# Softmax denominators behind the value products, and work moved between engines, in the mixers of a hybrid encoder layer

## The chip, the cores and the metric

The kernel runs on one core of a Trainium2 chip. The metric is device microseconds (us) of one execution, the median of several; less is better. A core has five engines with an instruction queue each: PE (matrix products, and transposes as products with the identity), DVE (elementwise and reductions), ACT (activation functions, copies with a scale), POOL (elementwise, and DMAs that accumulate) and SP, which in this kernel only issues DMAs. Each engine takes its instructions strictly in order and waits at semaphores, so an instruction that waits holds up everything behind it on its engine, DMA issues included. PSUM is the memory that PE writes to; here it is used as 8 banks of 128x512 fp32.

## The reference

One post-norm encoder layer over 1024 tokens of width 1024, in fp32. Two mixers share a projection, then come an output product, a norm, a SwiGLU feed-forward and a gated embedding. The part around the change, cut from the reference:

```python
u = x @ w_in                                    # rq, rk, rv, rg | aq, ak, av
kv = einsum('bhnsd,bhnse->bhnde', k * k_decay, v)   # retention, 8 heads, chunks of 128, both directions
...
y_ret = group_norm(y_fwd + y_bwd) * gn_gain * silu(rg)
scores = where(valid, q.k / 8 - slope * dist, -1e30)  # attention, 8 heads, window +-128
m = maximum(max(scores), sink)
e = exp(scores - m)
denom = sum(e) + exp(sink - m)
y_att = (e / denom) @ v
h = LN1(alpha * x + concat(y_ret, y_att) @ w_out)
```

## The kernel before

Every large product is written as three fp32r products of operands that are split into a high and a low part (`mm3`, L75 to L79: high by high, high by low, low by high). A split costs an ACT copy for the high part and a DVE subtraction for the low one (`split`, L69 to L72; `put`, L600 to L604, does both and stores the pair to DRAM).

The span of the profile falls into stages: the first projection (to about 48 us), the mixers (about 48 to 353 us), w_out, which is made as seven products of sums of blocks with operands that lie in DRAM as `wod` (from 353 us), LN1, and the feed-forward with its embedding gate (to the end). The change touches the mixers alone.

In the mixers the order of PE's work is written out by hand. A projection step (`take`) is one `mm3`, that is three 128x512 products; each step is a tick. Between the steps stand the mixers' own small products. `run` (L726) deals the two out against each other: attention group 0 runs first by itself, then retention group 0, then three pairs of a retention and an attention group i = 1, 2, 3, with 48 ticks each. Lists `later` and `side` hold functions that fire at a certain tick, so that work which depends on a result is put into the engines' queues some ticks after it. DVE, ACT, POOL and SP get their instructions in an order that a scheduler sets; `behind` (L81) ties an instruction to a place behind the last product.

A retention group turns its keys (L408), multiplies them with a decay for each direction (`keys`, L411, on DVE, from PSUM to SBUF), makes the chunk states (L428), scans them, scores (L459, L461), values (L481), and norms each half of 512 tokens: `evict` reads the sums out of PSUM (L488 and L489 squares on ACT, L490 a copy on DVE, L491 a subtraction on DVE), L498 sums the squares on PE, L500 makes a row on DVE, and then at 3, 6, 9, 12 and 15 ticks (`LAGS`) the row goes to 64 partitions by DMA (L505), POOL takes a power (L508), the result goes to DRAM (L511), comes back as a broadcast (L515), and DVE multiplies y by it (L519).

An attention group works on blocks of 128 queries, two heads at a time, each against two or three blocks of keys (`nk` = 256 or 384). POOL writes the sink logit into a column behind the scores (L545); PE makes the scores in a bank "s" (L548, L549); DVE scales them, adds the distances and takes the maximum (L550); DVE negates the maximum (L552); ACT takes the exponentials, the sink's column among them, and their sum (L554). Three ticks later (`LAG`) DVE takes the reciprocal of the sum (L558) and ACT multiplies the exponentials by it (L560). Then PE turns them into bank "t" (L572), ACT copies them out (L574, tile `ptr`), PE multiplies them with the values into bank "o" (L584), and after four blocks ACT copies the half out (L587). Banks "s", "t" and "o" are two each, so a product that starts in such a bank waits until the bank's last reader is done.

Beside this `presplit_out` (L606 to L643) makes the operands of w_out: it loads blocks of w_out into SBUF, adds blocks to each other in place on DVE (L638, in the order of the table `todo`), and stores each sum, split, with `put`. `presplit_gate` does the like for other weights (L653, L663).

Of the kernel before, what the change touches and what calls it, by code (L numbers as in the profile page):

```python
# [30 lines left out]
LAG = 3  # L31
# [11 lines left out]
def layer(tc, xT, xn, w_first, w_mt, w_rv, w_out, w_pg, w_pe, pT, w_gu, w_dn,  # L43
# [175 lines left out]
    nlg = cp.tile([P, 16], F32, name="nlg")  # L219
    dve.tensor_tensor(nlg, rr[:, 0:16], t_[:, 0:16], ALU.mult)  # L220
# [23 lines left out]
    def ev_aq(b, qs, h, i):  # L244
        sl = slice(h * HF, (h + 1) * HF)
        for g in range(2):
            sc_ = 0.125 / slope(i, g)
            a = slice(64 * g, 64 * g + 64)
            z = slice(64 * (1 - g), 64 * (1 - g) + 64)
            act.activation(qs[g][a, sl], b[a], AF.Copy, scale=sc_)  # L250
            dve.scalar_tensor_tensor(qs[g][z, sl], b[a], sc_, qs[g][a, sl].bitcast(F32), ALU.mult, ALU.subtract)
# [127 lines left out]
    def decay_k(i, h):  # L379
        e = bt([P, 2, P], "sq", 1)  # L380
        for d in range(2):
            behind(act.activation(e[:, d, :], cst[:, C_BASE + P:C_BASE + 2 * P], AF.Exp,
                                  scale=nlg[:, 8 * d + 2 * i + h:8 * d + 2 * i + h + 1]))
# [9 lines left out]
    class Retention:  # L393
# [8 lines left out]
        def keys(self, q):  # L402
# [7 lines left out]
            for d in range(2):  # L410
                dve.tensor_tensor(  # L411
                    kdec[:, d].rearrange("p n (h e) -> p n h e", h=2),
                    tb.rearrange("p n (h e) -> p n h e", h=2),
                    kd[:, d, 2 * i:2 * i + 2].unsqueeze(1).unsqueeze(3).to_broadcast([P, 4, 2, 64]),
                    ALU.mult)
# [69 lines left out]
        def evict(self, hh):  # L485
# [4 lines left out]
            dve.tensor_copy(self.half(hh), of)  # L490
# [35 lines left out]
    class Attention:  # L526


        def __init__(self, i, y):
            self.i, self.y, self.qs = i, y, pairs[i][2]  # L530
            self.st, self.sc, self.pt, self.o, self.ready = {}, {}, {}, {}, set()

        def scores(self, n):
# [9 lines left out]
            sc = self.sc[n] = [bt([P, NKT + 4], "sc", NSC) for _ in range(2)]  # L543
            for g in range(2):
                pool.tensor_copy(sc[g][:, nk:nk + 1], skb[:, 2 * i + g:2 * i + g + 1])  # L545
            for g in range(2):
# [4 lines left out]
                                         skb[:, 2 * i + g:2 * i + g + 1], ALU.add, ALU.max, st_[:, 0, j, g:g + 1])  # L551
            dve.tensor_scalar(st_[:, 1, j, :], st_[:, 0, j, :], -1.0, None, ALU.mult)  # L552
            for g in range(2):
                act.activation(sc[g][:, :nk + 1], sc[g][:, :nk + 1], AF.Exp, bias=st_[:, 1, j, g:g + 1],  # L554
                               accum_out=st_[:, 2, j, g:g + 1])

            def scaled():
                behind(dve.reciprocal(st_[:, 3, j, :], st_[:, 2, j, :]))  # L558
                for g in range(2):
                    behind(act.activation(sc[g][:, :nk], sc[g][:, :nk], AF.Copy, scale=st_[:, 3, j, g:g + 1]))  # L560
                self.ready.add(n)

            later.append((ticks[0] + LAG, scaled))

        def turn(self, n):
            assert n in self.ready
# [10 lines left out]
        def values(self, n):  # L577
# [8 lines left out]
            if j == 3:  # L586
                act.activation(self.half(hh), self.o[hh], AF.Copy)  # L587
# [6 lines left out]
    rnd = dr.tile([8, P, 8], F32, name="rnd")  # L594
    pgd = dr.tile([7, 4, P, 2, HF], F32, name="pgd")
# [28 lines left out]
    def presplit_out(kt, ops, start, gap, raws=()):  # L624
# [10 lines left out]
        def step(p, k, k2, i):  # L635
            x = hold[k]
            if k2 is not None:
                behind(dve.tensor_tensor(x, x, hold[k2], ALU.add))  # L638
            put(x, ops[i % len(ops)], wod[p - 1, kt])

        todo = ((1, 0, None), (2, 2, None), (3, 3, None), (5, 0, 1), (7, 1, 3), (6, 0, 3), (4, 0, 2))
        return [(ticks[0] + start, load)] + \
            [(ticks[0] + start + 5 + gap * i, lambda i=i, a=a: step(*a, i)) for i, a in enumerate(todo)]  # L643
# [1251 lines left out]
def const_table():  # L1895
# [10 lines left out]
    c[:, C_BASE:C_BASE + NKT] = np.where(d <= P, -d, np.float32(-1e33))  # L1906
# [68 lines left out]
```

## Time and profile before

| | |
|---|---|
| time, median of 3 runs | 1171.35 us (1170.49 to 1171.68) |
| span of the profiled execution | 1166.3 us |
| time around the span (median less span) | 5.05 us |
| PE busy | 1154.7 us, 99% of the span |
| DVE, ACT, POOL busy | 903.6, 576.1, 124.4 us |
| DVE busy in 150:250 us (mixers) | 83.7 of 100 us |
| ACT busy in 150:250 us | 69.8 of 100 us |
| PE's waits for others in the whole span | 3.1 us in four waits |

The profiled execution's own time is taken to be its span and the 5.05 us around it. Starts and durations are in us; an instruction's row gives start, duration, engine, line, operation, and output<-input by the program's names. In brackets stands how long the engine was idle ahead of it and what it waited for. Consecutive 128x512 products of PE overlap: they start 0.23 us apart though each lasts 0.39, so PE can stand still with hardly any idle time in a row; the distance between starts tells more. Rows of the queue view (SPq) are issues of DMAs; a DMA lands some us later.

### The profile page before, as it was taken

Reading aid. Unit: us, or ns where it says so; the run is one execution under the profiler, and the core shown is the slowest. Engines: PE = TensorE matmul, PEld = TensorE weight load, DVE = VectorE, ACT = ScalarE, POOL = GpSimd, SP = SyncE. Lnnn points to the kernel's source line nnn. Section 1 sums busy time; section 2 is a strip of 40 time slices with the busy share of each in tenths; the row PEclk is TensorE's granted clock in tenths of the full one; section 3 lists DMA queues with packets and bytes.
Section 4 is the critical chain, followed back from the end, with each engine's and each line's share of the span. In section 5 each row is a group of like instructions: output and inputs, shape, how many; then the busy total and the mean of one; then the engine's idle time right before and its main releaser. Section 6 shows DMA issues by size and latency. Waiting matters only on the chain.

```text
span 1166.3 us, 17917 instructions
## 1 busy us (share of the span) xinstructions
PE 1154.7 (99%) x6330; PEld 971.3 (83%) x6330; DVE 903.6 (77%) x1746; ACT 576.1 (49%) x1169; POOL 124.4 (11%) x182
## 2 busy tenths in 40 slices
PE   9999999999999999999999999999999999999997
PEld 7888888888887888888888888888888888888885
DVE  5666697877859788948999988889888976864678
ACT  5566358676756265214445433444344445552462
POOL 2001021202010020000000000000000020234243
PEclk9999999999999999999999999999999999999999
DMA  6345676646356955665232232232223289989978
GB/s 253 103 150 205 254 236 215 209 154 218 132 192 231 359 181 197 250 218 197 100 116 92 101 120 103 85 137 99 100 72 136 94 253 350 351 220 225 254 157 234
DMA packets 84377, 214.39 MB, mean 184 GB/s; under 512 B 12224, under 2 KB 17472, under 8 KB 84288
## 3 DMA queue, kind: packets, MB, share of 16 engines
q1 hardware_dynamic: 75504, 195.94, 47.6%
q0 software_dynamic: 8784, 17.31, 8.4%
q8 instruction: 50, 0.82, 0.3%
q14 instruction: 39, 0.32, 0.1%
HBM read 141.32 MB, written 62.16 MB: 174 GB/s over the span
## 4 chain that ended last, share of the span: by engine, by line
PE 94%; DVE 3%; DMA 1%; ACT 1%; issue 1%; POOL 0%; SPq 0%; DVEq 0%; POOLq 0%; ACTq 0%
PE bmm L802 8%; PE bmm L803 8%; PE bmm L804 8%; PE bt L802 6%; PE bt L803 6%; PE bt L804 6%; PE bmm L77 5%; PE bmm L78 5%; PE bmm L79 5%; PE bs L804 4%; PE bs L803 4%; PE bs L802 4%; PE bo L804 4%; PE bo L803 4%; PE bo L802 4%; PE bt L572 2%
## 5 line engine op out<-in xcount | busy, mean ns | idle before, releaser
L77 PE MATMUL bmm<-H,w 128*128 128x512 f32 x240 | 97.0, 404 | 0.0
L78 PE MATMUL bmm<-H,w 128*128 128x512 f32 x240 | 94.1, 392 | 0.0
L79 PE MATMUL bmm<-H,w 128*128 128x512 f32 x240 | 93.9, 391 | 0.0
L1561 POOL DMA_DIRECT2D h0b<-in_w_dn x24 | 21.6, 902 | 538.4 <-DVE ev L1367 503.6
L1387 ACT ACTIVATE ev<-ev 128x512 f32<-128x512 f32 x42 | 26.5, 631 | 103.7 <-DVE ev L1416 90.5
L77 PEld LDWEIGHTS bmm<-H,w 128*128 128x128 f32 x240 | 45.1, 188 | 11.0 <-issue 1.4
L79 PEld LDWEIGHTS bmm<-H,w 128*128 128x128 f32 x240 | 45.0, 188 | 10.2
L78 PEld LDWEIGHTS bmm<-H,w 128*128 128x128 f32 x240 | 45.1, 188 | 8.3 <-DVE H L72 0.4
L554 ACT ACTIVATE sc<-sc,st 128x385 f32<-128x385 f32 (+1 forms) x64 | 37.3, 586 | 27.1 <-DVE st L552 27.0
L550 DVE CUSTOM_DVE_ANT_0 sc<-cst,bs,skb 128x384 f32<-128x384 f32 (+1 forms) x64 | 34.9, 575 | 7.7 <-PE bs L549 7.4
L1416 DVE TENSOR_TENSOR ev<-ev,bt 128x512 f32<-128x512 f32 x44 | 30.1, 684 | 12.6 <-PE bt L804 12.5
L1367 DVE TENSOR_TENSOR ev<-ev,bs 128x256 f32<-128x256 f32 x63 | 25.6, 418 | 15.5 <-PE bs L804 14.7
L545 POOL COPY sc<-skb 128x1 f32<-128x1 f32 x64 | 17.4, 280 | 189.2 <-PE bt L572 163.2
L1389 DVE TENSOR_TENSOR ev<-ev 128x512 f32<-128x512 f32 x42 | 29.0, 691 | 10.6 <-ACT ev L1387 9.1
L802 PE MATMUL bmm<-H,u 128*128 128x512 f32 x92 | 36.1, 392 | 0.0
L803 PE MATMUL bmm<-H,u 128*128 128x512 f32 x92 | 36.0, 392 | 0.0
L804 PE MATMUL bmm<-H,u 128*128 128x512 f32 x92 | 35.8, 389 | 0.0
L71 ACT ACTIVATE H<-ln 128x512 fp32r<-128x512 f32 (+1 forms) x34 | 23.0, 679 | 24.1 <-DVE ln L1051 7.2
L560 ACT ACTIVATE sc<-sc,st 128x384 f32<-128x384 f32 (+1 forms) x64 | 34.2, 583 | 0.9 <-DVE st L558 0.9
L72 DVE TENSOR_TENSOR w<-raw,w 128x512 fp32r<-128x512 f32 x34 | 23.1, 688 | 13.9 <-ACT w L71 13.9
L574 ACT ACTIVATE ptr<-bt 128x384 f32<-128x384 f32 (+1 forms) x64 | 26.6, 458 | 12.9 <-PE bt L572 12.7
L802 PE MATMUL bmm<-H,w 128*128 128x512 f32 x84 | 32.9, 392 | 0.0
(802 smaller groups left out, 3903.0 us busy)
## 6 DMA issues: line engine op xcount, KB each, us to landing
ad<-ev SPq DMA_DIRECT2D x33, 512.0 KB, 2.6
pgd<-pro SPq DMA_DIRECT2D x28, 512.0 KB, 2.9
raw<-in_w_gu SPq DMA_DIRECT2D x22, 512.0 KB, 3.7
ln<-in_w_gu SPq DMA_DIRECT2D x22, 512.0 KB, 3.8
raw<-ad SPq DMA_DIRECT2D x40, 256.0 KB, 5.8
ln<-ad SPq DMA_DIRECT2D x37, 256.0 KB, 6.3
H<-in_w_dn SPq DMA_DIRECT2D x33, 256.0 KB, 7.1
wod<-aq SPq DMA_DIRECT2D x15, 512.0 KB, 2.7
```

The source lines that it names most:

```text
L77: pe.matmul(o, lh, rh, start=start, stop=False)
L78: pe.matmul(o, lh, rl, start=False, stop=False)
L79: recent[0] = pe.matmul(o, ll, rh, start=False, stop=stop).ins.name
L550: dve.tensor_tensor_reduce(sc[g][:, :nk], cst[:, tc0:tc0 + nk], b[:, :nk], slope(i, g), skb[:, 2 * i + g:2 * i + g + 1], ALU.add, ALU.max, ...
L554: act.activation(sc[g][:, :nk + 1], sc[g][:, :nk + 1], AF.Exp, bias=st_[:, 1, j, g:g + 1], accum_out=st_[:, 2, j, g:g + 1])
L560: behind(act.activation(sc[g][:, :nk], sc[g][:, :nk], AF.Copy, scale=st_[:, 3, j, g:g + 1]))
L574: act.activation(p_[:, :hi - lo, :], tb[:, :hi - lo, :], AF.Copy)
L802: pe.matmul(o, lh, rh, start=start, stop=False, skip_group_check=True)
L803: pe.matmul(o, lh, rl, start=False, stop=False, skip_group_check=True)
L804: pe.matmul(o, ll, rh, start=False, stop=stop, skip_group_check=True)
L1389: dve.tensor_tensor(c[:, 1, :], c[:, 0, :], c[:, 1, :], ALU.mult)
L1416: dve.tensor_tensor(get(name), ev[left][:, m, :], right, ALU.add)
```

## The change

Five parts, all in the mixers:

1. The probabilities stay unnormalised. The sink's column goes (64 copies on POOL), and so do the 32 reciprocals of one block and the 64 multiplications on ACT. Instead, once the fourth block of a half has its exponentials, `sums` at +3 ticks adds the exponential of sink less maximum (2 small ACT instructions) to the sums and takes one reciprocal for the four blocks on DVE; `store` at +5 ticks sends the reciprocals to DRAM with two DMAs, each of 128x4 single fp32 elements (L564 of the changed kernel), and `fetch` at +9 ticks brings them back as two broadcasts of 64x512 into the half of y (L568), from where DVE multiplies them with the value products as it empties bank "o" (L593, where ACT copied before). There are eight halves, so 16 stores and 16 fetches.
2. The scores are made with the opposite sign, distances positive and a minimum for the maximum, so that the exponential takes the minimum as it is (scale -1): the 32 negations on DVE go.
3. The keys' decay goes from DVE (16 instructions 128x512) to ACT (32 of 128x4x64, L413 of the changed kernel).
4. `evict` copies on ACT (L488 of the changed kernel) instead of DVE, 8 times.
5. w_out's sums are made by 16 DMAs from POOL's queue that load a block and add it to the tile (L643 of the changed kernel), instead of 16 additions on DVE, in another order of `todo`.

The diff, cut to its core:

```diff
-LAG = 3
+LAGA = (3, 5, 9)
...
-            sc_ = 0.125 / slope(i, g)
+            sc_ = -0.125 / slope(i, g)
...
             for d in range(2):
-                dve.tensor_tensor(
-                    kdec[:, d].rearrange("p n (h e) -> p n h e", h=2),
-                    tb.rearrange("p n (h e) -> p n h e", h=2),
-                    kd[:, d, 2 * i:2 * i + 2].unsqueeze(1).unsqueeze(3).to_broadcast([P, 4, 2, 64]),
-                    ALU.mult)
+                for h in range(2):
+                    e = slice(64 * h, 64 * h + 64)
+                    act.activation(kdec[:, d, :, e], tb[:, :, e], AF.Copy, scale=kd[:, d, 2 * i + h:2 * i + h + 1])
...
-            dve.tensor_copy(self.half(hh), of)
+            act.activation(self.half(hh), of, AF.Copy)
...
-            sc = self.sc[n] = [bt([P, NKT + 4], "sc", NSC) for _ in range(2)]
-            for g in range(2):
-                pool.tensor_copy(sc[g][:, nk:nk + 1], skb[:, 2 * i + g:2 * i + g + 1])
+            sc = self.sc[n] = [bt([P, NKT], "sc", NSC) for _ in range(2)]
...
-                                         skb[:, 2 * i + g:2 * i + g + 1], ALU.add, ALU.max, st_[:, 0, j, g:g + 1])
-            dve.tensor_scalar(st_[:, 1, j, :], st_[:, 0, j, :], -1.0, None, ALU.mult)
+                                         nskb[:, 2 * i + g:2 * i + g + 1], ALU.add, ALU.min, st_[:, 0, j, g:g + 1])
             for g in range(2):
-                act.activation(sc[g][:, :nk + 1], sc[g][:, :nk + 1], AF.Exp, bias=st_[:, 1, j, g:g + 1],
+                act.activation(sc[g][:, :nk], sc[g][:, :nk], AF.Exp, bias=st_[:, 0, j, g:g + 1], scale=-1.0,
                                accum_out=st_[:, 2, j, g:g + 1])
-
-            def scaled():
-                behind(dve.reciprocal(st_[:, 3, j, :], st_[:, 2, j, :]))
+            if j < 3:
+                return
+            home = adn[2 * i + hh]
+            r = self.y[:, hh * HF:(hh + 1) * HF]
+
+            def sums():
                 for g in range(2):
-                    behind(act.activation(sc[g][:, :nk], sc[g][:, :nk], AF.Copy, scale=st_[:, 3, j, g:g + 1]))
-                self.ready.add(n)
-
-            later.append((ticks[0] + LAG, scaled))
+                    behind(act.activation(st_[:, 1, :, g], st_[:, 0, :, g], AF.Exp, bias=skb[:, 2 * i + g:2 * i + g + 1]))
+                behind(dve.tensor_tensor(st_[:, 2], st_[:, 2], st_[:, 1], ALU.add))
+                behind(dve.reciprocal(st_[:, 3], st_[:, 2]))
+
+            def store():
+                for g in range(2):
+                    sp.dma_start(home[g].rearrange("j q -> q j"), st_[:, 3, :, g])
+
+            def fetch():
+                for g in range(2):
+                    sp.dma_start(r[64 * g:64 * g + 64], home[g].rearrange("j q -> (j q)").partition_broadcast(64))
+
+            later.extend((ticks[0] + at, f) for at, f in zip(LAGA, (sums, store, fetch)))
...
             if j == 3:
-                act.activation(self.half(hh), self.o[hh], AF.Copy)
+                dve.tensor_tensor(self.half(hh), self.o[hh], self.half(hh), ALU.mult)
...
-        def step(p, k, k2, i):
-            x = hold[k]
-            if k2 is not None:
-                behind(dve.tensor_tensor(x, x, hold[k2], ALU.add))
-            put(x, ops[i % len(ops)], wod[p - 1, kt])
+        def add(k, k2):
+            behind(pool.dma_start(hold[k], w_out[kt + 4 * (k2 // 2)][:, (k2 % 2) * HF:(k2 % 2 + 1) * HF], accum_op=ALU.add))
...
-        todo = ((1, 0, None), (2, 2, None), (3, 3, None), (5, 0, 1), (7, 1, 3), (6, 0, 3), (4, 0, 2))
+        todo = ((1, 0), (2, 2, (0, 1)), (5, 0), (3, 3, (0, 3), (1, 3)), (6, 0), (7, 1, (0, 2)), (4, 0))
```

PE's instructions and their order are the same in both kernels. How the other engines' queues move is shown at three places. In the rows a name is a tile and its number in the program (numbers differ between the two kernels), with the line ahead and the size behind; "x2" is two in a row.

First place: DVE in pair i = 2, from the last maximum of attention's first block to the decay of retention's scores. Tiles st are attention's maxima and sums, kv the retention's states, qq its queries, pt its decayed scores out of banks bs. Before:

```order
L552 TENSOR_SCALAR st_2363<-st_2363 128x2
L558 RECIPROCAL st_2363<-st_2363 128x2
L436 COPY kv_2403<-bt_2405 128x256
L464 TENSOR_TENSOR qq_2452<-rq_1947,qd_2080 128x512
L436 COPY kv_2403<-bt_2422 128x192
L464 TENSOR_TENSOR qq_2452<-rq_1947,qd_2080 128x512
L441 SCALAR_TENSOR_TENSOR kv_2403<-kv_2403,cd 128x64
L444 SCALAR_TENSOR_TENSOR kv_2404<-kv_2404,cd 128x64
L441 SCALAR_TENSOR_TENSOR kv_2403<-kv_2403,cd 128x64
L444 SCALAR_TENSOR_TENSOR kv_2404<-kv_2404,cd 128x64
L461 TENSOR_TENSOR pt_2439<-bs_2440,dt_2081 128x512
L461 TENSOR_TENSOR pt_2439<-bs_2441,dt_2081 128x512
```

The same stretch of DVE in the changed kernel (y is the attention output of pair 1, emptied out of bank bo):

```order
L593 TENSOR_TENSOR y_1578<-bo_2159,y_1578 128x512
L434 COPY kv_2346<-bt_2348 128x256
L462 TENSOR_TENSOR qq_2395<-rq_1903,qd_2029 128x512
L434 COPY kv_2346<-bt_2365 128x192
L462 TENSOR_TENSOR qq_2395<-rq_1903,qd_2029 128x512
L439 SCALAR_TENSOR_TENSOR kv_2346<-kv_2346,cd 128x64
L442 SCALAR_TENSOR_TENSOR kv_2347<-kv_2347,cd 128x64
L439 SCALAR_TENSOR_TENSOR kv_2346<-kv_2346,cd 128x64
L442 SCALAR_TENSOR_TENSOR kv_2347<-kv_2347,cd 128x64
L459 TENSOR_TENSOR pt_2382<-bs_2383,dt_2030 128x512
L459 TENSOR_TENSOR pt_2382<-bs_2384,dt_2030 128x512
```

The negation and the reciprocal ahead of the states' copy are gone, and the multiplication of a finished attention half stands there instead.

Second place: ACT in pair i = 3, around the blocks whose exponentials (tile sc) were normalised. Before:

```order
L574 ACTIVATE ptr_3228<-bt_3225 128x256
L574 ACTIVATE ptr_3233<-bt_3230 128x256
L554 ACTIVATE sc_3197,st_3083<-sc_3197,st_3083 128x385
L554 ACTIVATE sc_3198,st_3083<-sc_3198,st_3083 128x385
L560 ACTIVATE sc_3197<-sc_3197,st_3083 128x384
L560 ACTIVATE sc_3198<-sc_3198,st_3083 128x384
L554 ACTIVATE sc_3235,st_3083<-sc_3235,st_3083 128x385
L554 ACTIVATE sc_3236,st_3083<-sc_3236,st_3083 128x385
```

After:

```order
L549 ACTIVATE sc_3112,st_3004<-sc_3112,st_3004 128x384
L549 ACTIVATE sc_3113,st_3004<-sc_3113,st_3004 128x384
L71 ACTIVATE w_3221<-raw_3219 128x512
L580 ACTIVATE ptr_3137<-bt_3134 128x256
L580 ACTIVATE ptr_3142<-bt_3139 128x256
L549 ACTIVATE sc_3144,st_3004<-sc_3144,st_3004 128x384
L549 ACTIVATE sc_3145,st_3004<-sc_3145,st_3004 128x384
L609 ACTIVATE aq_2963<-raw_3021 128x512
```

The two normalisations behind the exponentials are gone; the first pair of exponentials here (sc_3112, the tiles of sc_3197 before) now stands ahead of the copies of ptr, and nothing of ACT lies between it and the transposes that read it.

Third place: SP at the end of the mixers. sn, rnd, kv and rb are the norm's row on its way to DRAM and back for the last retention group, adn and y the denominators' way, w and u the first operands of w_out's products, ped a store of another weight. Before:

```order
L515 DMA kv_3565<-rnd 64x512 x2
L813 DMA w_3833<-wod 128x1024
L604 DMA ped<-aq_3046 128x1024
L505 DMA sn_3719<-kv_3717 64x1x8 x2
L511 DMA rnd<-sn_3719 128x8
L604 DMA ped<-aq_3046 128x1024
L515 DMA rb_3720<-rnd 64x512 x2
L813 DMA u_3835<-wod 128x1024
L813 DMA w_3837<-wod 128x1024
L813 DMA u_3839<-wod 128x1024
```

After:

```order
L513 DMA kv_3455<-rnd 64x512 x2
L611 DMA ped<-aq_2963 128x1024
L568 DMA y_2269<-adn 64x512
L503 DMA sn_3608<-kv_3606 64x1x8 x2
L823 DMA w_3722<-wod 128x1024
L611 DMA ped<-aq_2963 128x1024
L509 DMA rnd<-sn_3608 128x8
L513 DMA rb_3609<-rnd 64x512 x2
L823 DMA u_3724<-wod 128x1024
L823 DMA w_3726<-wod 128x1024
L823 DMA u_3728<-wod 128x1024
```

One of the fetches of the denominators now stands ahead of the norm's spread (sn), and the first load for w_out has moved behind it.

18 lines of the change are left out of this document (11 added, 7 removed).

## The prediction

> **What bounds the kernel now.** The page comes first: its span and busy times.
>
> ```profile
> span 1166.3 us, 17917 instructions
> PE 1154.7 (99%) x6330; PEld 971.3 (83%) x6330; DVE 903.6 (77%) x1746; ACT 576.1 (49%) x1169; POOL 124.4 (11%) x182
> ```
>
> PE is busy all the time, and the change leaves its products and their order as they are. So the time can fall only by what PE stands still for, and rise by any new standstill. The view of waits, for PE:
>
> ```profile
> PE bo L142 <- POOL sq L139: 1.3, 1, 1.3
> PE bt L802 <- ACT h0b L971: 1.1, 1, 1.1
> PE bs L548 <- DVE pt L461: 0.5, 1, 0.5
> PE bt L572 <- ACT sc L560: 0.2, 1, 0.2
> ```
>
> The first lies in the start, ahead of the change. The other three lie in the mixers or just behind them, and each has DVE or ACT, the relieved engines, at its end. That is all there is to win, and the timeline says how much, by the distance between starts of products (0.23 us where PE runs freely). The three places in turn:
>
> ```profile
> 232.25 0.39 PE L78 MATMUL bmm<-H,w 128*128 128x512 f32 x1
> 232.48 0.39 PE L79 MATMUL bmm<-H,w 128*128 128x512 f32 x1
> 233.34 0.44 PE L548 MATMUL bs<-k,aq 128*128 128x384 f32 x1 [0.47 <-DVE pt L461]
> ...
> 299.14 0.39 PE L79 MATMUL bmm<-H,w 128*128 128x512 f32 x1
> 299.71 1.05 PE L572 MATMUL bt<-cst,sc 128*128 128x128 f32 x6 [0.17 <-ACT sc L560]
> ...
> 363.38 0.39 PE L804 MATMUL bs<-u,H 128*128 128x512 f32 x1
> 364.87 0.50 PE L802 MATMUL bt<-w,H 128*128 128x512 f32 x1 [1.09 <-ACT h0b L971]
> ```
>
> Lost are 0.86 - 0.23 = 0.63 us, 0.57 - 0.23 = 0.34 and 1.49 - 0.23 = 1.26, together 2.23 us or 0.19% of the time. About 0.2% (2.34 us) is also what a measurement of this kernel can tell from no change.
>
> **The change part by part.** The sum stands against the profiled execution's own time, 1166.3 + 5.05 around it = 1171.35 us, which is the median.
>
> *The stall at 233.34* (bank "s" not yet read by L461). DVE ahead of it:
>
> ```profile
> 229.55 0.17 DVE L558 RECIPROCAL st<-st 128x2 f32<-128x2 f32 x1 [1.23 <-ACT sc L554]
> 230.01 0.42 DVE L436 COPY kv<-bt 128x256 f32<-128x256 f32 x1 [0.29 <-issue]
> ...
> 232.60 1.28 DVE L461 TENSOR_TENSOR pt<-bs,dt 128x512 f32<-128x512 f32 x2
> ```
>
> From 230.01 on DVE is without a gap, and it starts so late because the reciprocal stands in its queue and waits 1.23 us for ACT's exponential. Negation and reciprocal go; in their place comes the multiplication of a finished half, which waits for value products and a fetch:
>
> ```profile
> 227.27 0.61 PE L584 MATMUL bo<-ptr,av 128*64 128x128 f32 x8
> L490 DVE COPY y<-bo 128x512 f32<-128x512 f32 x8 | 5.5, 690 | 5.9 <-ACT pt L489 4.9 <-ACT kv L489 1.0
> ```
>
> The products end at 227.88, a pass over a bank costs 0.69 (L490 is the nearest row), so L436 can start near 228.7, 1.3 us earlier, and the stall needs only 0.63. Gain 0.63; nothing if the fetch is late.
>
> *The stall at 299.71.* The transposes wait for the normalised tile:
>
> ```profile
> 299.04 1.12 ACT L560 ACTIVATE sc<-sc,st 128x384 f32<-128x384 f32 x2 [0.43 <-DVE st L558]
> ```
>
> These two instructions go, here and in 31 other places (at 1.12 us a pair up to 36 us of ACT). Gain 0.34. Next late there is the second exponential, which ended ahead of 299.04, over half a microsecond before PE starts now.
>
> *The stall at 364.87.* It hangs on a chain that begins in the last retention norm:
>
> ```profile
> 336.84 0.33 SPq L813 DMA_DIRECT2D w<-wod  x1
> 338.16 1.44 SPq L505 DMA_DIRECT2D sn<-kv  x2
> 345.71 1.10 SPq L515 DMA_DIRECT2D rb<-rnd  x2
> ...
> 348.80 0.69 DVE L723 SCALAR_TENSOR_TENSOR y<-sq,y 128x512 f32<-128x512 f32 x1
> 350.27 0.75 DVE L519 SCALAR_TENSOR_TENSOR y<-y,gn,rb 128x512 f32<-128x512 f32 x1 [0.78 <-DMA rb<-rnd]
> ```
>
> DVE waits 0.78 us for rb, then works without a gap to 365, and ACT's L971, for which PE stands, follows it. So this stall moves one to one with the landing of rb, by 0.78 at the best, since L723 ends at 349.49. Before, the spread (sn) was queued behind a 512 KB load, w; now that load comes after it. Its landing here and as a median over the mixers, in the view of DMAs:
>
> ```profile
> sn<-kv SPq DMA_DIRECT2D x2, 2.0 KB, 3.9
> sn<-kv SPq DMA_DIRECT2D x16, 2.0 KB, 2.8
> ```
>
> 1.1 us earlier would give the whole 0.78. Against it stands one fetch of the denominators that SP now issues just ahead. Bounds 0.78 and a small loss; I take 0.6, by the rows of sn.
>
> *Keys' decay and the evict copy.* Nearest rows:
>
> ```profile
> L434 ACT ACTIVATE kv<-bt 128x256 f32<-128x256 f32 x4 | 1.5, 378 | 0.7 <-DVE kv L436 0.7
> L411 DVE TENSOR_TENSOR qq<-bt,kd 128x512 f32<-128x512 f32 x8 | 5.5, 684 | 0.1
> L587 ACT ACTIVATE y<-bo 128x512 f32<-128x512 f32 x8 | 4.8, 595 | 4.9 <-PE bo L584 4.9
> ```
>
> One call of `keys` becomes 4 x 0.378 = 1.51 us of ACT for 2 x 0.684 = 1.37 of DVE, 12.1 us in all against the 36 or so that ACT loses; the 8 copies of `evict` (0.595) take the place of the 8 that moved to DVE. Both engines end with less: DVE loses 16 x 0.684 here, 16 more in w_out's sums, and the small ones. Cost nothing, as other ACT and DVE work between PE's products hides it; uncovered, 0.14 us a call.
>
> The Trainium skill, page "ScalarE: Activation LUTs", section Rules for kernel authors, advises against this part: additions and multiplications belong on VectorE, not ScalarE. The rows above do not agree for fp32 out of PSUM: 0.595 us on ACT stands against 0.690 on DVE. If the rule held for the keys and nothing hid them, the sum would lose 8 x 0.14 = 1.1 us.
>
> *Denominators' trip.* Two stores of single 4-byte elements and two fetches a half. No such store is in the trace. The nearest rows are the norm's store and broadcast, and the queue's packets in two short windows, one that held only the norm's store, and one of bulk loads:
>
> ```profile
> rb<-rnd SPq DMA_DIRECT2D x8, 128.0 KB, 3.9
> rnd<-sn SPq DMA_DIRECT2D x8, 4.0 KB, 1.6
> q1 hardware_dynamic: 144, 0.00, 9.7%
> q1 hardware_dynamic: 274, 1.01, 101.3%
> ```
>
> The windows are 0.8 and 2.5 us long, so a small packet costs 0.097 x 16 x 0.8 / 144 = 8.6 ns and a bulk one 1.013 x 16 x 2.5 / 274 = 148 ns. A store has 512 elements, 32 for each of 16 engines: 0.3 us by the small price, 4.7 by the bulk one, on the 1.6 of landing. I take 2.2, nearest to the small store, with 6.3 as the other end. Time for it: four ticks.
>
> ```profile
> L77 PE MATMUL bmm<-H,w 128*128 128x512 f32 x240 | 97.0, 404 | 0.0
> ```
>
> 240 ticks in 305 us of mixers make 1.27 us a tick, 5.1 for four. SP then fetches without waiting. The tightest use is the half of pair 1 whose multiplication stands ahead of L461:
>
> ```profile
> 196.33 0.32 SPq L604 DMA_DIRECT2D pgd<-pro  x1
> 200.51 1.28 DVE L461 TENSOR_TENSOR pt<-bs,dt 128x512 f32<-128x512 f32 x2
> 202.52 0.42 PE L548 MATMUL bs<-k,aq 128*128 128x384 f32 x1
> ```
>
> The second fetch stands behind this pgd store on SP: issued about 196.7, it lands at 200.6 by the 3.9; multiplication 0.6 and L461 0.69 more end at 201.9, ahead of 202.52. Margin 0.6. Cost 0, with under 1 us as the other end.
>
> *w_out's sums.* DVE loses 16 x 0.68; the puts on ACT now wait for an accumulating DMA. Its landing, minimum, median, maximum, from the down projection's:
>
> ```profile
> DMA to landing us min/median/max: 4.5/6.7/8.7
> 87.37 0.84 ACT L574 ACTIVATE ptr<-bt 128x384 f32<-128x384 f32 x2
> 91.70 1.53 PE L584 MATMUL bo<-ptr,av 128*64 128x128 f32 x24
> ```
>
> Queued behind such a put on ACT are the copies of ptr and exponentials; a pair of ptr copies ended at 88.21 and was read at 91.70, so ACT may stand 3.5 us unseen. The sums are issued some us ahead; the stage that these landings are from runs beside many other accumulating loads, the mixers beside none, so I take the lower ones, and no cost; the other end is a rival.
>
> Sum: 1171.35 - 0.63 - 0.34 - 0.6 = **1169.8 us**, from 1169.3 to 1170.8 by its own bounds.
>
> **The rivals.**
>
> *More goes than the rows show.* Besides these three PE has small delays of a tenth that no row attributes, and the 0.78 may come in full: 2.23 to 2.6 us gone, 1168.8. For it speaks that both engines lose work wherever PE waits for them; against it that L723 bounds the third stall.
>
> *Nothing is won.* The stalls only change hands: the exponential, the multiplication or the longer SP queue is as late as what it replaces. 1171.3.
>
> *Slower: the 4-byte stores are slow.* If their elements cost the bulk price, the second store lands up to 1.6 + 2 x 4.7 = 11 us after its issue, and SP, in order, stands at the fetch up to 6 us with weight stores and loads behind it. In pair 1 DVE then stands at the multiplication, L461 comes late, and PE waits at 202.52 for all beyond 0.6 us. Held by 4.5 us that is 3.9 lost; the other gains of 0.97 stay: 1174.3. It decides against the forecast from a fetch 2.2 us late on. The row of 8.6 ns speaks against it, but that is of 32-byte elements. The Trainium skill ("DMA: Bandwidth & Descriptors", Specifications) says that transfers under 512 B are not at line rate but read, modified and written; no run here shows it for 4 bytes.
>
> *Slower by the accumulating DMAs.* At landings of 8.7 us ACT stands beyond its 3.5 us at some of the 16 sums; 8 times 0.5 us less the gains gives about 1173.8.
>
> **How the numbers follow.** Forecast 0.40, nothing won 0.15 (both within 0.2%, 1169.0 to 1173.7: 0.55); more than the rows 0.22 (faster by over 0.2%); slow stores 0.13 and slow sums 0.10 (slower: 0.23). The range leaves out the ends of the outer cases: 1168.3 to 1174.1.
>
> **What would show it.** In the profile after: PE's waits at L544 for DVE's pt and at L578 for sc gone; rb landing before 349.5 and the standstill near 364 down to about 0.5 us; stores of adn landing in 2 to 3 us; no row in which PE waits for DVE's L459 near 202, or for ptr. Wrong it would be with any new wait of PE above 1 us in the mixers, or with the stall near 364 grown, which would mean that SP's longer queue delays rb.

## The result, and the profile after

The changed kernel takes 1240.9 us (median of 4 runs, 1239.35 to 1244.61) against 1170.92 us of the kernel before on the same chip: a ratio of 1.060, 95% interval 1.0587 to 1.0617. It is 70 us slower. 1169.8 had been forecast, and 1174.3 was the worst of the rivals.

The page of the changed kernel begins:

```profile
span 1237.5 us, 17742 instructions
PE 1175.6 (95%) x6330; PEld 983.5 (79%) x6330; DVE 878.0 (71%) x1666; ACT 562.1 (45%) x1153; POOL 121.6 (10%) x134
```

DVE and ACT are relieved, as forecast (by 26 and 14 us). PE has as many products as before and yet 71 us more of span. Where they lie is read from the windows. The columns are length, then PE, PEld (PE's loading of weights), DVE, ACT and POOL, each with its busy time and, in brackets, the count of its rows, then PE's granted clock, the DMA engines' busy share and GB/s. Stretches with as many rows of PE can be set beside each other. Before:

```profile
50.00:358.00 308.00, 307.36 (x2203) 256.68 (x2203) 226.19 (x518) 197.34 (x458) 40.32 (x86) 1.00 0.58 200
358.00:1166.00 808.00, 798.65 (x3924) 676.42 (x3922) 649.79 (x1179) 351.25 (x667) 74.99 (x81) 1.00 0.56 178
```

After:

```profile
50.00:430.00 380.00, 328.63 (x2204) 269.21 (x2203) 201.90 (x440) 184.96 (x444) 39.18 (x42) 0.94 0.74 179
430.00:1237.00 807.00, 798.52 (x3923) 676.15 (x3922) 648.75 (x1177) 350.11 (x665) 74.30 (x81) 1.00 0.57 178
```

The same 2200 products of the mixers take 380 us instead of 308: all of the loss, and the rest of the kernel is as it was (807 us and 808). The view of waits, for PE (total, times, longest):

```profile
PE bt L578 <- ACT ptr L580: 17.3, 6, 5.6
PE bo L590 <- ACT ptr L580: 17.0, 4, 9.4
PE bs L544 <- DVE pt L459: 13.5, 4, 7.1
PE bmm L77 <- ACT rk L235: 3.0, 1, 3.0
PE bo L142 <- POOL sq L139: 1.3, 1, 1.3
PE bmm L77 <- DVE aq L251: 0.4, 1, 0.4
PE bt L812 <- ACT h0b L981: 0.3, 1, 0.3
```

Some 51 us of new waits stand on ACT and DVE, which are both less busy than before, so these engines must wait for something themselves. One place shows for what, in the first attention group. SP's issues:

```profile
78.94 0.32 SPq L611 DMA_DIRECT2D wod<-pro  x1
79.31 1.36 SPq L564 DMA_DIRECT2D adn<-st  x2
82.03 0.33 SPq L611 DMA_DIRECT2D wod<-aq  x1
92.87 1.11 SPq L568 DMA_DIRECT2D y<-adn  x2
```

The two stores of the denominators go out at 79.31. From about 82.4 SP stands until 92.87 at the fetch that needs them. ACT at the same time:

```profile
84.35 0.19 ACT L549 ACTIVATION_READ_ACCUMULATOR sc<-sc,st 128x1 f32 x1
92.75 0.63 ACT L609 ACTIVATE pro<-raw 128x512 fp32r<-128x512 f32 x1 [8.21 <-DMA wod<-pro]
93.29 0.86 ACT L580 ACTIVATE ptr<-bt 128x384 f32<-128x384 f32 x2
```

ACT's next put may not write its buffer before the 512 KB store that was issued at 78.94, ahead of the denominators, has landed. It lands 13.7 us after its issue, and the copies of ptr, for which PE waits, stand behind that put. So it is not one transfer that is slow but everything that is under way beside it. Over the whole of the mixers ACT's waits for such landings grew, as two kinds of put show. Before:

```profile
ACT aq L602 <- DMA wod<-aq: 1.4, 1, 1.4
ACT pro L602 <- DMA pgd<-pro: 2.8, 4, 1.3
```

After:

```profile
ACT aq L609 <- DMA wod<-aq: 27.2, 7, 14.2
ACT pro L609 <- DMA pgd<-pro: 20.7, 7, 7.8
```

The DMA queues in two stretches, 81 to 82 us and 84 to 91 us:

```profile
DMA packets 1022, 0.06 MB, mean 63 GB/s; under 512 B 1006, under 2 KB 1006, under 8 KB 1022
```

```profile
DMA packets 96, 0.17 MB, mean 25 GB/s; under 512 B 54, under 2 KB 54, under 8 KB 96
```

In the first, nearly all of the 1024 small packets of both stores (1006 rows) pass within a microsecond. In the second, next to nothing moves for seven microseconds, 25 GB/s of the 200 that the mixers had before. The landing of the 16 stores, and what became of bulk stores beside them:

```profile
DMA to landing us min/median/max: 10.8/11.4/18.2
```

```profile
wod<-pro SPq DMA_DIRECT2D x6, 512.0 KB, 7.3
adn<-st SPq DMA_DIRECT2D x16, 2.0 KB, 11.4
```

2 KB take 11.4 us, and the six w_out stores from pro 7.3 by the median, instead of the 2.6 of before. No store of the denominators lands in less than 10.8, so each of the eight halves makes such a jam, of about 9 us where it was read.

The waits add up to 51 of 71 us. The other 20 fit PE's clock, 0.94 over 380 us. PE's rows around one of the long waits:

```profile
118.31 0.88 PE L590 MATMUL bo<-ptr,av 128*64 128x128 f32 x12
123.14 1.06 PE L590 MATMUL bo<-ptr,av 128*64 128x128 f32 x8 [3.96 <-ACT ptr L580]
124.13 0.80 PE L77 MATMUL bmm<-A,H 128*128 128x512 f32 x1
124.73 0.63 PE L78 MATMUL bmm<-A,H 128*128 128x512 f32 x1
125.15 0.63 PE L79 MATMUL bmm<-A,H 128*128 128x512 f32 x1
125.58 0.63 PE L77 MATMUL bmm<-A,H 128*128 128x512 f32 x1
...
127.26 0.39 PE L78 MATMUL bmm<-A,H 128*128 128x512 f32 x1
127.48 0.39 PE L79 MATMUL bmm<-A,H 128*128 128x512 f32 x1
```

After 4 us of standing, eight small products take 1.06 us where twelve took 0.88, and the large ones start 0.43 us apart instead of 0.23 until about 127, so a long wait is paid for once more behind its end. The Trainium skill ("TensorE: Matmul & The Clock Gate", Part 1) describes this: after an idle window of about 3.4 us the clock is halved, and it is full again after about as long of sustained work. The trace agrees: the products are slow from 123.14 to about 127, 3.9 us.

ACT stood at this place for one of the accumulating loads from POOL's queue (part 5), which the jam held up as well:

```profile
121.61 0.63 ACT L609 ACTIVATE aq<-states 128x512 fp32r<-128x512 f32 x1 [7.84 <-DMA states<-in_w_out]
```

### The profile page after: what moved, and what is told of

Same layout as the page of the kernel before. It is cut to its first block, busy times and chain, and to the rows that moved or that the text cites. A ratio compares the mean times of both kernels' runs of the same rounds, so it can differ in the third digit from the quotient of the medians.

```text
span 1237.5 us, 17742 instructions
## 1 busy us (share of the span) xinstructions
PE 1175.6 (95%) x6330; PEld 983.5 (79%) x6330; DVE 878.0 (71%) x1666; ACT 562.1 (45%) x1153; POOL 121.6 (10%) x134
## 4 chain that ended last, share of the span: by engine, by line
PE 73%; DMA 15%; DVE 6%; ACT 3%; issue 1%; SPq 1%; POOL 0%; DVEq 0%; ACTq 0%; POOLq 0%
PE bmm L812 7%; PE bmm L813 7%; PE bmm L814 7%; PE bt L812 6%; PE bt L813 6%; PE bt L814 6%; PE bs L814 4%; PE bs L813 4%; PE bs L812 4%; PE bo L814 3%; PE bo L813 3%; PE bo L812 3%; DMA pgd<-pro 3%; DMA wod<-aq 2%; DMA wod<-pro 2%; PE bmm L77 2%
## 5 line engine op out<-in xcount | busy, mean ns | idle before, releaser
L77 PE MATMUL bmm<-H,w 128*128 128x512 f32 x240 | 101.4, 422 | 3.7 <-ACT rk L235 3.0
L78 PE MATMUL bmm<-H,w 128*128 128x512 f32 x240 | 97.9, 408 | 0.0
L79 PE MATMUL bmm<-H,w 128*128 128x512 f32 x240 | 97.2, 405 | 0.0
L77 PEld LDWEIGHTS bmm<-H,w 128*128 128x128 f32 x240 | 47.7, 199 | 16.6 <-ACT rk L235 3.4
L79 PEld LDWEIGHTS bmm<-H,w 128*128 128x128 f32 x240 | 47.5, 198 | 11.1
L78 PEld LDWEIGHTS bmm<-H,w 128*128 128x128 f32 x240 | 47.6, 198 | 9.0 <-DVE H L72 0.3
L549 ACT ACTIVATE sc<-sc,st 128x384 f32<-128x384 f32 (+1 forms) x64 | 37.2, 585 | 16.4 <-DVE st L546 16.4
L578 PE MATMUL bt<-cst,sc 128*128 128x128 f32 x176 | 26.8, 285 | 17.3 <-ACT ptr L580 17.3
L546 DVE CUSTOM_DVE_ANT_0 sc<-cst,bs,nskb 128x384 f32<-128x384 f32 (+1 forms) x64 | 35.0, 575 | 10.1 <-PE bs L545 10.0
L590 PE MATMUL bo<-ptr,av 128*64 128x128 f32 x352 | 25.5, 283 | 17.0 <-ACT ptr L580 17.0
L578 PEld LDWEIGHTS bt<-cst,sc 128*128 128x128 f32 x176 | 21.2, 145 | 24.0 <-ACT ptr L580 19.8
L610 DVE TENSOR_TENSOR pro<-pre,pro 128x512 fp32r<-128x512 f32 x28 | 19.6, 699 | 27.2 <-ACT pro L609 26.9
L590 PEld LDWEIGHTS bo<-ptr,av 128*64 128x64 f32 x352 | 20.5, 139 | 22.1 <-ACT ptr L580 18.4
L544 PE MATMUL bs<-k,aq 128*128 128x384 f32 (+1 forms) x64 | 23.8, 378 | 13.5 <-DVE pt L459 13.5
```

Of the source, the lines that this page charges most:

```text
L77: pe.matmul(o, lh, rh, start=start, stop=False)
L78: pe.matmul(o, lh, rl, start=False, stop=False)
L79: recent[0] = pe.matmul(o, ll, rh, start=False, stop=stop).ins.name
L546: dve.tensor_tensor_reduce(sc[g][:, :nk], cst[:, tc0:tc0 + nk], b[:, :nk], slope(i, g), nskb[:, 2 * i + g:2 * i + g + 1], ALU.add, ALU.min ...
L549: act.activation(sc[g][:, :nk], sc[g][:, :nk], AF.Exp, bias=st_[:, 0, j, g:g + 1], scale=-1.0, accum_out=st_[:, 2, j, g:g + 1])
L578: pe.transpose(tb[:, kb, :], self.sc[n][g][:, kb * P:(kb + 1) * P], ident)
```

## The experiments

Theory 1: the 4-byte stores jam the DMA engines, and all that is queued or under way lands later. Theory 2: it is SP, standing in order at the fetch. Theory 3: the cost lies in other parts of the change. The first four kernels tell these apart, each timed beside the kernel before.

**rows16.** The reciprocals lie in SBUF so that the four of one partition and head are neighbours, and are stored as 16-byte runs; their order in DRAM is then not the one that the output needs.

```diff
-                behind(dve.reciprocal(st_[:, 3], st_[:, 2]))
+                behind(dve.reciprocal(rec.rearrange("p (g j) -> p j g", g=2), st_[:, 2]))
...
-                    sp.dma_start(home[g].rearrange("j q -> q j"), st_[:, 3, :, g])
+                    sp.dma_start(home[g].rearrange("j q -> (j q)").rearrange("(p e) -> p e", e=4), rec[:, 4 * g:4 * g + 4])
```

> The changed kernel, with each half's reciprocals stored as 16-byte runs (128 packets a store instead of 512 of 4 bytes), so that the fetched numbers stand in another order than the computation needs; nothing else differs. Theory 1 (the 4-byte stores jam the DMA engines: their 1024 writes a half need about 9 us, and all that is queued behind lands as much later): the stores land in 2 to 4 us instead of 11.4, PE's new waits of about 50 us go nearly all, time 1169 to 1178 us. Theory 2 (SP stands in order at the fetch and holds the rest up): the same, as the fetch waits less. Theory 3 (the cost lies in the accumulating DMAs or in the keys' decay on ACT): stays above 1225 us.

Measured: 1173.3 us, ratio 1.0029 (1.0018 to 1.0040); the stores land as follows.

```profile
DMA to landing us min/median/max: 1.4/3.7/5.7
```

67 of the 70 us are gone by the form of one kind of small store. Theory 3 falls as an account of the 70 us. Three microseconds are left, which is looked into below.

**half_store.** One head's store is left out, and both fetches read the other's.

```diff
             def store():
-                for g in range(2):
+                for g in range(1):
...
-                    sp.dma_start(r[64 * g:64 * g + 64], home[g].rearrange("j q -> (j q)").partition_broadcast(64))
+                    sp.dma_start(r[64 * g:64 * g + 64], home[0].rearrange("j q -> (j q)").partition_broadcast(64))
```

> The changed kernel, storing the reciprocals of one head of the two only; both fetches read that one, so the second head's half is multiplied by the wrong numbers. Half of the 4-byte packets. Theory 1: a half's jam falls from about 9 us to 4 or 5, and buffers hide some of it, so the loss of 70 us falls to 15 to 35: 1186 to 1206 us. Theory 2: the same direction, the SP stand falls alike. Theory 3: stays above 1225 us.

Measured: 1222.3 us, ratio 1.045 (1.042 to 1.048). The landing:

```profile
DMA to landing us min/median/max: 10.2/10.7/10.9
```

A miss for all three theories as they were put: with half of the 4-byte writes the jam is nearly as long, and 52 of the 70 us stay. The writes of the two stores hardly queue up behind each other; something within one store takes the 10 us.

**before_store.** The kernel before, with the stores alone, into a tile that nothing reads.

```diff
             later.append((ticks[0] + LAG, scaled))
+            if j == 3:
+
+                def store():
+                    for g in range(2):
+                        sp.dma_start(adn[2 * i + hh][g].rearrange("j q -> q j"), st_[:, 3, :, g])
+
+                later.append((ticks[0] + 5, store))
```

> The kernel before, with the two 4-byte stores a half added at the same tick, into a DRAM tile that nothing reads. No fetch, so SP never stands for the stores' landing. Theory 1: the jam is there without the fetch, 1210 to 1240 us. Theory 2: no more than 1180 us. Theory 3: no more than 1173 us, as none of the other parts is in it.

Measured: 1225.3 us, ratio 1.047 (1.045 to 1.048), landing:

```profile
DMA to landing us min/median/max: 8.8/10.6/12.1
```

Sixteen stores of 2 KB that nobody waits for cost 55 us. So the jam is enough by itself, without a fetch. In the changed kernel SP does stand for the stores, 73 us in nine waits:

```profile
SPq L568 <- DMA adn<-st: 73.0, 9, 10.5
```

What this adds (theory 2) was not measured by itself; if the costs simply add up, it is a part of the remaining 15 us, which the other parts share.

**flip.** A whole version without small writes: PE turns the 128x8 reciprocals, ACT copies them, and one DMA stores 8 rows of 512 bytes.

```diff
-LAGA = (3, 5, 9)
+LAGA = (3, 5, 6, 9)
...
+            t8 = bt([8, P], "t8", 1)
+
+            def flip():
+                tb = bank("t", (P, 4, P))
+                pe.transpose(tb[:8, 0, :], rec, ident)
+                behind(act.activation(t8, tb[:8, 0, :], AF.Copy))
+
             def store():
-                for g in range(2):
-                    sp.dma_start(home[g].rearrange("j q -> q j"), st_[:, 3, :, g])
+                sp.dma_start(home.rearrange("g j q -> (g j) q"), t8)
```

> The changed kernel, with the reciprocals of a half turned on PE (one transpose of 128x8 a half), copied by ACT and stored as 8 rows of 512 bytes in one DMA; the fetch as it was. The computation is whole. Theories 1 and 2: the stores land in about 2 us, PE's new waits go, and the three old stalls (2.2 us) are partly gone: 1168.5 to 1172 us. Theory 3: stays above 1225 us.

Measured: 1175.7 us, ratio 1.0043 (1.0027 to 1.0058). The jam is gone, but the time is 3.7 us above the range of theories 1 and 2, and far from theory 3. The profile is of the slowest of the five runs (1178.4 us). PE's waits:

```profile
PE bt L567 <- ACT pro L616: 2.9, 1, 2.9
PE bt L585 <- ACT t L568: 2.5, 2, 1.8
PE bs L544 <- DVE pt L459: 1.0, 1, 1.0
```

and ACT ahead of the first of them (L616 is the put):

```profile
104.01 0.63 ACT L616 ACTIVATE aq<-states 128x512 fp32r<-128x512 f32 x1 [3.70 <-DMA states<-in_w_out]
```

ACT stood 3.7 us for an accumulating DMA of part 5. The turn itself costs too: its copy on ACT holds a bank "t" (the second wait).

The runs that follow ask what in the small writes is slow, and what the other parts are worth. Theory A: the number of separate 4-byte writes costs, wherever they go. Theory B: writes into the same short stretch of DRAM hinder each other.

**rows4.** The changed kernel, the same single elements, with the four of a partition next to each other in DRAM.

```diff
-                    sp.dma_start(home[g].rearrange("j q -> q j"), st_[:, 3, :, g])
+                    sp.dma_start(home[g].rearrange("j q -> (j q)").rearrange("(p e) -> p e", e=4), st_[:, 3, :, g])
```

> The changed kernel with the same 512 single 4-byte elements a store, but laid down in DRAM so that the four of a partition stand in one 16-byte run (neighbouring bytes are written by one DMA engine, not by many); the fetched numbers stand in another order than the computation needs. Theory A (the number of separate 4-byte writes costs, some 9 ns each for all engines together, wherever they go): as the changed kernel, 1235 to 1245 us, landing near 11 us. Theory B (writes of different engines into the same short stretch of DRAM hinder each other): landing well below 8 us and a time below 1205 us.

Measured: 1234.3 us, ratio 1.055 (1.052 to 1.057), landing 8.1 us by the median. The time is nearly that of the changed kernel, as theory A has it; the landing lies between the two theories.

**before_spread.** As before_store, but the elements 512 bytes apart.

```diff
-                        sp.dma_start(adn[2 * i + hh][g].rearrange("j q -> q j"), st_[:, 3, :, g])
+                        sp.dma_start(adn[2 * i + hh][g].rearrange("j q e -> q j e")[:, :, 0:1], st_[:, 3, :, g:g + 1])
...
+    adn = dr.tile([8, 2, 4, P, P], F32, name="adn")
```

> The kernel before with the 4-byte stores added, unread, each element now 512 bytes from the next in DRAM, beside the 1225.3 us of the same with elements 4 bytes apart. Theory A: the same landing near 10.6 us and 1220 to 1230 us. Theory B: the landing falls to 2 to 4 us and the time to 1170 to 1180 us.

Measured: 1172.4 us, ratio 1.0018 (1.0007 to 1.0028), and the landing of as many 4-byte writes:

```profile
DMA to landing us min/median/max: 1.8/2.7/3.9
```

Theory A falls: neither the number of writes nor their size makes the jam by itself, but how near they lie to each other.

**before_pitch64, before_pitch16, before_cluster.** The same with the elements 64 bytes apart (the tile's last size 16 for P), 16 bytes apart (4 for P), and with the four of a partition next to each other in groups 512 bytes apart.

```diff
+                        sp.dma_start(adn[2 * i + hh][g][:, 0:4], st_[:, 3, :, g])
...
+    adn = dr.tile([8, 2, P, P], F32, name="adn")
```

> The kernel before with the unread 4-byte stores, elements 64 bytes apart in DRAM: the case between 4 bytes (landing 10.6 us, 1225 us) and 512 bytes (2.7 us, 1172 us). If the delay grows with how many writes fall into one short stretch, of 64 bytes or so: landing 2 to 3.5 us and 1170 to 1175 us. If all writes into the same 512 bytes or the same 32 KB hinder each other as much as neighbours do: landing over 8 us, over 1210 us.

> The kernel before with the unread 4-byte stores, elements 16 bytes apart in DRAM: four in each 64 bytes, 32 in each 512. If the delay goes by the number of writes in some 64 bytes: between the landings of 2.7 us (one) and 10.6 us (sixteen), near 4.3 us by a straight line, time 1172 to 1185 us, and the same as the groups of four. If it goes by stretches of 512 bytes and more: as this, but the groups of four faster.

> The kernel before with the unread 4-byte stores, the four elements of a partition next to each other, and these groups 512 bytes apart: four in 64 bytes, four in 512. If the delay goes by the number of writes in some 64 bytes: as with elements 16 bytes apart. If by stretches of 512 bytes and more: near 2.9 us and 1172 us. If it takes different engines at neighbouring bytes: near 2.7 us too.

Measured, with the other layouts of the same 512 elements a store:

| writes in each 64 bytes (in 512 bytes) | kernel | landing, median us | time us, ratio |
|---|---|---|---|
| 1 (1) | before_spread | 2.7 | 1172.4, 1.0018 |
| 1 (8) | before_pitch64 | 2.7 | 1172.0, 1.0015 (1.0002 to 1.0028) |
| 4 (32) | before_pitch16 | 4.3 | 1183.2, 1.010 (1.004 to 1.016) |
| 4 (4) | before_cluster | 4.9 | 1184.2, 1.011 (1.007 to 1.015) |
| 16 (128) | before_store | 10.6 | 1225.3, 1.047 |

The landings with four in 64 bytes, first even and then in groups:

```profile
DMA to landing us min/median/max: 3.5/4.3/5.3
```

```profile
DMA to landing us min/median/max: 3.6/4.9/6.7
```

The groups have an eighth of the writes in each 512 bytes and are no faster, and elements 64 bytes apart land no later than elements 512 bytes apart, so the stretch that counts is about 64 bytes; 32 is not excluded. With even spacing each further write into the same 64 bytes adds about (10.6 - 2.7) / 15 = 0.53 us. Different stretches go side by side: 512 writes into 512 of them land in 2.7 us, and half_store, with half as many stretches to fill, had nearly the same landing as both stores. The price is not the same in every layout: (4.9 - 2.7) / 3 = 0.73 us in before_cluster, and in the changed kernel some (8.1 - 2.7) / 15 = 0.36 in rows4, which also has sixteen in 64 bytes; rows16, with four writes of 16 bytes in each, landed in 3.7. Whether it takes different DMA engines at neighbouring bytes is open: before_cluster speaks against it if, as was assumed, one engine writes the four elements of a partition, which no view here shows. What the memory does in these 0.5 us is not shown by any run either.

**pool_store.** The changed kernel, with the 4-byte stores from POOL's queue.

```diff
-                    sp.dma_start(home[g].rearrange("j q -> q j"), st_[:, 3, :, g])
+                    pool.dma_start(home[g].rearrange("j q -> q j"), st_[:, 3, :, g])
```

> The changed kernel with the 4-byte stores issued from POOL's queue instead of SP's. Theory A and B, if what is jammed are the DMA engines or the memory, which both queues share: hardly better, 1225 to 1245 us. If what is jammed is SP's own ring of descriptors, in which the weights' stores and loads stand behind: below 1200 us.

Measured: 1299.6 us, ratio 1.110 (1.108 to 1.112), landing 10.2 us. This is outside both expected ranges. Another queue does not help; SP's ring is not what is jammed. PE's waits for DVE's L459 are 33.0 us here and 13.5 in the changed kernel; why it is 59 us slower in all was not followed up.

**noden, noden_noadd, flip_noadd, before_add.** What the other parts are worth. noden is the changed kernel without part 1:

```diff
-            sc = self.sc[n] = [bt([P, NKT], "sc", NSC) for _ in range(2)]
+            sc = self.sc[n] = [bt([P, NKT + 4], "sc", NSC) for _ in range(2)]
+            for g in range(2):
+                pool.tensor_copy(sc[g][:, nk:nk + 1], nskb[:, 2 * i + g:2 * i + g + 1])
...
+            def scaled():
+                behind(dve.reciprocal(st_[:, 3, j, :], st_[:, 2, j, :]))
+                for g in range(2):
+                    behind(act.activation(sc[g][:, :nk], sc[g][:, :nk], AF.Copy, scale=st_[:, 3, j, g:g + 1]))
...
-                dve.tensor_tensor(self.half(hh), self.o[hh], self.half(hh), ALU.mult)
+                act.activation(self.half(hh), self.o[hh], AF.Copy)
```

noden_noadd and flip_noadd have w_out's sums on DVE again besides, with the old table; before_add is the kernel before with the new `add` and table alone.

> The changed kernel with part 1 undone: probabilities normalised on ACT as before, sink column by POOL; parts 2 to 5 (negated scores, keys' decay and evict copy on ACT, sums by accumulating DMAs) stay. The computation is whole. If parts 2 to 5 do what the forecast said of them: the stall of DVE's L461 partly gone, 1169 to 1171.5 us. If the accumulating DMAs or the keys on ACT cost: 1173 us and more, with PE waiting for ACT's copies of ptr or for kdec.

> Parts 2, 3 and 4 alone (negated scores, keys' decay and evict copy on ACT); normalisation and w_out's sums as in the kernel before. The computation is whole. If the accumulating DMAs hold up ACT's puts and so give back a part of the gain: 1167.8 to 1169.3 us, faster than with them (1169.2). If they are free: 1169 to 1171 us.

> The version that turns the reciprocals on PE and stores 512-byte rows, with w_out's sums back on DVE. The computation is whole. If what made that version 5 us slower than the kernel before is ACT standing for accumulating DMAs (2.9 us seen at one place): 1170 to 1173 us. If it is the turn itself (its bank, its copy on ACT, its fetch): 1174 to 1176 us.

> The kernel before with part 5 alone: w_out's sums by accumulating DMAs in the new order. The computation is whole. As the forecast had it, no cost: 1168.5 to 1171 us. If ACT stands at the puts for their landing beyond what its work ahead hides: 1172 to 1176 us, with PE waiting for ACT's copies of ptr.

| kernel | parts of the change | time us | ratio (95% interval) |
|---|---|---|---|
| noden | 2, 3, 4, 5 | 1169.2 | 0.9992 (0.9981 to 1.0003) |
| noden_noadd | 2, 3, 4 | 1166.7 | 0.9961 (0.9948 to 0.9975) |
| flip | 1 (512-byte rows), 2, 3, 4, 5 | 1175.7 | 1.0043 (1.0027 to 1.0058) |
| flip_noadd | 1 (512-byte rows), 2, 3, 4 | 1170.0 | 0.9996 (0.9987 to 1.0005) |
| before_add | 5 | 1168.9 | 0.9990 (0.9978 to 1.0003) |

Parts 2, 3 and 4 alone make the kernel 0.39% faster, and this is the fastest version. PE's waits there:

```profile
PE bo L142 <- POOL sq L139: 1.3, 1, 1.3
PE bmm L77 <- DVE aq L251: 1.1, 1, 1.1
PE bt L798 <- ACT h0b L967: 0.3, 1, 0.3
```

Its 1166.7 us is below both expected ranges. The stalls on L461 and on the normalised tile are gone, and that behind the mixers is down to 0.3, though here the normalisation is still on ACT. With part 5 beside them the gain is lost (noden), and flip is 0.5% above flip_noadd, each against the kernel before on its own chip; alone on the kernel before part 5 changes nothing that can be told. So its cost depends on what stands near it, and not on ACT's standing alone, which is much the same in noden and in before_add:

```profile
ACT aq L598 <- DMA states<-in_w_out: 10.8, 3, 4.2
ACT aq L602 <- DMA states<-in_w_out: 8.2, 3, 4.7
```

In noden no wait of PE names these puts, so how the loss reaches PE there stays open. Part 1 in the form of flip, with harmless stores but with the turn, costs some 0.35% (flip_noadd against noden_noadd) for an ACT that had time.

## Why the prediction was wrong, point by point

- *What bounds the kernel* was right: PE's order, and any new standstill of PE is paid in full. What it left out is that a standstill of some microseconds is paid again in clock.
- *The three stalls* went, but the reasons given hold for one of them only. The one behind the mixers fell from 1.1 to 0.3 us, in the changed kernel too, and DVE no longer waited for rb, with w queued behind sn; the same came with part 5 alone (before_add). That on L461 was to go with the reciprocal, and that on the normalised tile with the normalisation; in noden_noadd both are gone with the normalisation still on ACT and the reciprocal still ahead of the states' copy on DVE, which waited 0.82 us at it. So that these two went is not explained by what the forecast named, and was luck as far as the runs show. In the changed kernel the waits for a normalised tile are gone, but those for DVE's L459 grew to 13.5 us in four.
- *Keys' decay and the evict copy* were set at nothing, and the rule of the Trainium skill that was weighed there ("ScalarE: Activation LUTs", Rules for kernel authors) at 1.1 us. The keys' size was off: a quarter of a call takes 0.47 us and not 0.378 (the rows stand below the list), so a call takes 1.9 us on ACT against 1.37 on DVE. For these multiplications the rule's order is right, and only the copies are faster on ACT. ACT had the time all the same: with part 2 these parts brought 0.39% (4.6 us by the ratio, 3.8 between the medians), more than the 2.2 us that the stalls of the profiled execution made up. Part of the difference is that this execution was a quick one: the runs of the kernel before beside the experiments lie 2.1 us above their spans, not 5.05, so their median of 1170.5 has a span of about 1168.4, some 2 us more than the one that was read. Which of the three parts brings the gain was not tried.
- *The denominators' trip* is the step that failed. It took 2.2 us for a store, "nearest to the small store, with 6.3 as the other end", and a cost of 0 with under 1 us as the other end. The store took 11.4. The price of a packet was nearly right: 64.5% of 16 engines over 1 us for 1018 packets is 10 ns, against 8.6. Wrong was to count packets at all: the 32-byte elements of the nearest row put 2 writes into 64 bytes, these 16, and what a store takes goes by the writes in one stretch, about 0.53 us for each further one. The rival of slow stores had the direction, but priced it by bulk packets, two stores one after the other, and as a delay of one fetch at one place; that its 11 us for the landing agree with the 11.4 is luck, since one store alone takes 10.7 (half_store). What it did not have is that nearly all transfers under way stand as long, eight times, and that ACT's puts wait for those.
- *The time for the trip* was misread too. The 240 products on L77 are of the whole span and of one kind only; in the mixers that view gives 224 of them, and `take` counts the 64 steps that make rv (rows `bmm<-A,H`, `bmm<-pt,H` and `bmm<-qq,H`) as well, so 288 ticks in 305 us, 1.06 us a tick and 4.2 for four. With the store at 11.4 this decided nothing. Nor did the sum's lower bound: the terms at their best (0.63, 0.34, 0.78) give 1169.6, not 1169.3.
- *The rule of the Trainium skill* that was weighed there ("DMA: Bandwidth & Descriptors", Specifications: under 512 B not at line rate but read, modified and written) points the right way and does not tell the cases apart: 4-byte writes 64 bytes from each other land in 2.7 us, next to each other in 10.6. No run shows whether the slow ones are read, modified and written.
- *w_out's sums* were set at nothing, with 3.5 us of ACT that nobody would see. Alone that holds (before_add), though ACT stood up to 4.7 us there. Beside the other parts they cost 0.3 to 0.5%, 3.6 to 5.5 us by the ratios, about the size of that rival; in flip one place is seen, the one at 104.01, where ACT stood 3.7 us and PE 2.9.

The rows of the keys' decay in the changed kernel (shortest, median and longest in ns), a quarter of a call each:

```profile
L413 ACT ACTIVATE qq<-bt,kd x16: 452/462/475, 134.2 to 331.8; 128x256 f32<-128x256 f32 x16
L413 ACT ACTIVATE pt<-bt,kd x16: 458/478/501, 136.8 to 334.3; 128x256 f32<-128x256 f32 x16
```

## What to carry to other kernels

A small store is not cheap because it is small: what counted here is how many separate writes fall into the same 64 bytes of DRAM, and a store that scatters a column over a row, 4 bytes at a time, held up nearly all transfers of the core for some ten microseconds. Turn the data first, or write at least 64 bytes apart (how dear it is to read such a spread row back was not tried). Even then the trip has to earn its place: with the data turned, flip_noadd is as fast as the kernel before and not faster. When an engine that has less to do than before is suddenly late, look at what its next instruction's buffer is waiting for. When a price is taken from the nearest row, ask in what the two differ besides size.

## What the runs showed of the hardware

- 512 writes of 4 bytes from one DMA land after 2.7 us when no two fall into the same 64 bytes of DRAM, 4.3 to 4.9 with four, 8.1 (rows4) to 10.6 (before_store) with sixteen; two such DMAs at once take about as long as one (10.6 in before_store, 10.7 for the single one of half_store).
- Meanwhile bulk transfers of the same core hardly move: 25 GB/s over 7 us. A 512 KB store from SP's queue lands after 13.7 us, and ACT stood 7.8 us for an accumulating load from POOL's.
- The same layout stored from POOL's queue lands in 10.2 us.
- A multiplication of 128x256 fp32 from PSUM by a scale per partition takes 0.46 to 0.48 us on ACT, one of 128x512 0.68 on DVE; a copy of 128x512 takes 0.595 on ACT and 0.690 on DVE.
